# Small transfers of the inverse and of the sample step: from SyncE's DMA queue to GpSimd's

## The chip, the cores and the metric

The kernel runs on one core of one Trainium2 chip. The metric is the device time of one execution in microseconds (us). TensorE (PE) multiplies, VectorE (DVE) and ScalarE (ACT) do elementwise work, GpSimd (POOL) does some copies and issues DMAs, SyncE (SP) only issues DMAs.

## The reference, cut to what matters

Two layers of a hybrid decoder trunk over 256 prompt tokens and 8 sample tokens (264 columns in all). Each layer projects the normalised activations with one matrix, runs three branches on the result and projects back:

```python
for l in range(2):
    z = rms_norm(x) @ w_in[l]            # 2048 -> 3200 + 3072 + 1024 columns
    a = rwkv_time_mix(z[..., :3200], state_wkv[l], ...)   # 12 heads x 64, delta-rule matrix state
    b = attention_branch(z[..., 3200:6272], caches[l])    # 3 groups of 4 heads, windows 128, 512, 2048
    c = pool_branch(z[..., 6272:], state_pool[l])
    x = x + concat(a, b, c) @ w_out[l]   # 2048 -> 2048

def step(S, inp):                        # time mixing, one token
    sa = einsum('bhvk,bhk->bhv', S, -kk_t)
    S = S * w_t + sa[..., None] * (kk_t * a_t) + v_t[..., None] * k_t
    return S, einsum('bhvk,bhk->bhv', S, r_t)
```

The prompt's 256 time-mixing steps are done in four chunks of 64, which needs the inverse of a triangular 64x64 matrix for each of 12 heads and 4 chunks. The 8 sample tokens take one step each, from states in memory. Outputs are the activations, the new states and the new keys and values.

## The kernel before, in words

All weights are float32 in HBM. `stream` (L327 has its matmuls) loads them as 292 quarters of 512 KB (`raw`, three buffers, SP's queue, L155), ScalarE rounds each to `hi` (two buffers, L137), VectorE makes the rest `lo` = raw - hi (three buffers, L140), and 24 matmuls into `acc` read them: 7008 in all, 3504 a layer. Everything else on TensorE, here called side products, goes between these matmuls, into `a`. `w_out` is the last part of each layer's stream; its first quarter reads mb[1] and mb[2], the gated outputs of attention groups 1 and 2.

Time mixing in `a_solve`: chunk Gram matrices `gs` are stored to `g_dram`; the diagonal 32x32 blocks are loaded back as `xm`, with one row per block, and solved on VectorE column by column (`rm`, `tm`, 15 steps). The 16x16 inverses go through `rat_dram`, `ra_dram`, `rbt_dram` and `rb_dram` into the layout in which `invert` merges them on TensorE (product(x16, rat), then product(y16, right), then product(x32, rbt) and product(y32, rb)). x16 and x32 come back from `x_dram` and `x12_dram` in `load_x`. The result is stored in i22, i11 and i12 and loaded as `rt` by `inverses` for the chunk chain `turn`.

The sample step in `a_sample` spreads r, w, k and the others over partitions through `sk_dram` and `sv_dram`, loads them as `svec` and `sval`, updates the state in six pieces `s` (loaded and stored on GpSimd's queue, L158), and brings the output back through `so_dram` as `aos`. The sample attention stores its queries to `q_dram` and loads them as `qb`; keys and values come from the caches as `kc` and `vc`. In each group the products `a<-vc,ppad` feed VectorE's `ex` and `os`, ScalarE's `os`, two transposes on TensorE (L118), then `osb`, `sgb` and `mb`. GpSimd also copies the sample columns of queries, keys and values to `compb` (L855).

`dma` issues on SP (L155), `dma2` on GpSimd (L158). The order of instructions on each engine is not the order of the code: class `Plan` schedules the whole list with its own costs and dependences, and writes out one order for each engine, which the engine then keeps. A changed queue therefore moves other work too. `Plan` charges an issue on GpSimd's queue to GpSimd itself, and lets it land later than one on SP's.

Of the kernel before, what the change touches and what calls it, by code (L numbers as in the profile page):

```python
# [19 lines left out]
P = 128  # L20
# [83 lines left out]
class Trunk:  # L104
# [370 lines left out]
    def a_solve(self):  # L475

        ap = self.apool
        self.wc = ap.tile([P, 6, NCH], F32, tag="wc", name=self.nm("wc"))
        self.nc.gpsimd.tensor_copy(self.wc, self.wp[:, :, :, CH])
        xm, rm = (self.qpool.tile([P, 1056], F32, tag="s4", bufs=2, name=self.nm(s)) for s in ("xm", "rm"))  # L480
        tm = ap.tile([P, 768], F32, tag="k3", bufs=4, name=self.nm("tm"))
        mask = self.c("mask").unsqueeze(1).to_broadcast([P, NCH, P])
        for t0 in (0, 3):
            gs = [ap.tile([P, NH, P], F32, tag="gs", name=self.nm("gs"), bufs=2) for _ in UROWS]
            for i in range(3):
                pg = [self.ps("a") for _ in UROWS]
                with self.bundle(140):
                    for cidx in range(NCH):
                        for o, hr in zip(pg, UROWS):
                            self.mm(o[:, cidx * P:(cidx + 1) * P], self.bk[hr, t0 + i, cidx, :], self.ar[hr, t0 + i, cidx, :])  # L490
                for g, o in zip(gs, pg):
                    self.tt(g[:, 4 * i:4 * i + 4, :], o.rearrange("p (c n) -> p c n", n=P), mask, ALU.mult)
            for par, g in enumerate(gs):
                g0 = par * 6 + t0
                self.dma(self.g_dram[:, g0:g0 + 3].rearrange("p t c n -> p (t c n)"), g.rearrange("p h n -> p (h n)"))
                lo = slice(64 * par, 64 * par + 32)
                self.dma(self.x12_dram[4 * g0:4 * g0 + 12].rearrange("h s t -> s h t"), g[lo, :, 96:128])
        n = 96
        for blk in range(2):
            for par in range(2):  # L500
                r0, c0, q0 = 64 * par + 32 * blk, 64 + 32 * blk, 48 * blk + 24 * par
                self.dma(xm[q0:q0 + 24, :1024].rearrange("q (s x) -> q s x", x=32),
                         self.g_dram[r0:r0 + 32, 6 * par:6 * par + 6, :, c0:c0 + 32].rearrange("s t c x -> (t c) s x"))
        self.dma(self.x_dram, xm[:n, :1024])
        self.load_x()
        for par, hr in enumerate(UROWS):
            for t0 in (0, 3):
                g0 = par * 6 + t0
                self.dma(self.g_dram[hr, g0:g0 + 3].rearrange("p t c n -> p (t c) n")[:, :, 64:128],
                         self.ar[hr, t0:t0 + 3].rearrange("p t c n -> p (t c) n")[:, :, 64:128])  # L510
        view = lambda a: a[:n].rearrange("p (u x) -> p u x", u=2)[:, :, :512].rearrange("p u (s t) -> p u s t", t=32)[:, :, :, :16]
        X, R = view(xm), view(rm)
        self.nc.vector.memset(rm, 0.0)
        self.nc.vector.memset(rm[:, 0:1024:33], 1.0)
        for t in range(1, 16):
            tv = tm[:n, :2 * t * t].rearrange("p (u c s) -> p u c s", u=2, s=t)
            col = X[:, :, 0:t, t:t + 1].rearrange("p u s o -> p u o s").to_broadcast([n, 2, t, t])
            self.tt(tv, R[:, :, 0:t, 0:t], col, ALU.mult)
            self.red(R[:, :, 0:t, t:t + 1], tv)
        self.act(X.rearrange("p u s t -> p u t s"), R)  # L520
        for blk in range(2):
            rows = slice(48 * blk, 48 * blk + 48)
            self.dma(self.rat_dram[:, 1 - blk], X[rows, 0])
            self.dma(self.ra_dram[:, 1 - blk], R[rows, 1])
        self.nc.gpsimd.memset(xm[:48, :512].rearrange("p (s t) -> p s t", t=32)[:, :, 16:32], 0.0)
        self.dma(self.rbt_dram.rearrange("q s t -> q (s t)"), xm[:48, :1024])
        self.dma(self.rb_dram.rearrange("q s t -> q (s t)"), rm[48:96, :1024])

    def invert(self):

# [10 lines left out]
        self.dma(rbt, self.rbt_dram.rearrange("(g j) r t -> (j r) g t", j=4))  # L541
        self.dma(rb, self.rb_dram.rearrange("(g j) r t -> (j r) g t", j=4))
# [13 lines left out]
        p = product(self.x16, rat, 16)  # L556
# [9 lines left out]
        self.dma(self.i22_dram.rearrange("(g j) r t -> (j r) g t", j=4), rb)  # L566
# [5 lines left out]
        self.dma(self.i11_dram.rearrange("(i k) s j t -> (k s) i (j t)", k=4), inv[:, 0].rearrange("p (i n) -> p i n", i=3))  # L572
        p = product(y32, rb, 32)
        self.act(inv[:, 1].rearrange("p (g t) -> p g t", t=32), p)
        self.dma(self.i12_dram.rearrange("(g j) r t -> (j r) g t", j=4), inv[:, 1].rearrange("p (g t) -> p g t", t=32))

    def load_x(self):
        self.x16 = self.apool.tile([P, 12, 32], F32, tag="st", name=self.nm("x16"), bufs=2)
        self.x32 = self.apool.tile([P, 12, 32], F32, tag="st", name=self.nm("x32"), bufs=2)
        self.nc.gpsimd.memset(self.x16, 0.0)  # L580
        for j in range(4):
            for u in range(2):
                o = 32 * j + 16 * u
                src = self.x_dram[48 * (1 - u):48 * (1 - u) + 48].rearrange("(g j) (r c) -> j r g c", j=4, c=32)
                self.dma(self.x16[o:o + 16, :, 16 * u:16 * u + 16], src[j, 0:16, :, 16:32])
        self.dma(self.x32, self.x12_dram.rearrange("(g j) r c -> (j r) g c", j=4))

    def a_chain(self):

# [58 lines left out]
    def inverses(self):  # L648

        rt = self.apool.tile([P, 6, NCH, 64], F32, tag="rt", name=self.nm("rt"))  # L650
        flat = rt.rearrange("p t c n -> p (t c) n")
        for par in range(2):
            lo, hi = slice(64 * par, 64 * par + 32), slice(64 * par + 32, 64 * par + 64)
            self.nc.gpsimd.memset(flat[hi, :, 0:32], 0.0)
            for cidx in range(NCH):
                self.dma(rt[lo, :, cidx, 0:32], self.i11_dram[6 * par:6 * par + 6, :, cidx, :].rearrange("g s x -> s g x"))
            for d, r in ((self.i22_dram, hi), (self.i12_dram, lo)):
                self.dma(flat[r, :, 32:64], d[24 * par:24 * par + 24].rearrange("h s t -> s h t"))
        return rt

    def rows(self, cidx):
# [118 lines left out]
    def a_sample(self):  # L780
# [10 lines left out]
        self.dma(v[:, 0:48], self.sv_dram.rearrange("n e -> (n e)").rearrange("(p x) -> p x", p=P))  # L791
        src = I["state_wkv"][l].rearrange("b h v k -> (b h v k)").rearrange("(p x) -> p x", p=P)
        dst = self.outs["s_wkv"][l].rearrange("b h v k -> (b h v k)").rearrange("(p x) -> p x", p=P)
        nv = 8
        for pc in range(48 // nv):
            if pc % 2 == 0:
                vec = sp.tile([P, 5, 64], F32, tag="arows", name=self.nm("svec"))
                self.dma(vec, self.sk_dram.rearrange("q n r e -> q (n r) e").rearrange("q (p g) e -> g p q e", g=3)[pc // 2])
# [18 lines left out]
        self.dma(self.so_dram.rearrange("n e -> (n e)").rearrange("(p x) -> p x", p=P), out)  # L817
        os_ = sp.tile([112, 64], F32, tag="aos", name=self.nm("aos"))
        sa = v[:112, 0:64]
        self.nc.vector.memset(os_[32:64], 0.0)  # L820
        for par in range(2):
            self.dma(os_[64 * par:64 * par + 48], self.so_dram.rearrange("(n q) e -> q n e", q=2)[par])
# [1005 lines left out]
```

## Time and profile before

| | us |
|---|---|
| median of 3 runs | 1066.29 (1060.89, 1066.29, 1066.63) |
| profiled execution | 1064.51 |
| its span, first to last instruction | 1062.7 |
| TensorE busy | 1040.7 (98%) |
| VectorE busy | 856.7 (81%) |
| ScalarE busy | 546.7 (51%) |
| GpSimd busy | 141.7 (13%) |

The granted TensorE clock was 0.998 of full speed over the execution, the 2.4 GHz level. DMA-issuing instructions are not counted as busy, so GpSimd's and SP's share is more than the table shows. The profiled execution's time lies within the three runs. In layer 0 the column-by-column solve runs around 165 to 200 us, the inverse's first product on TensorE starts at 211.1 us and `w_out` at 442.84; in layer 1 the last two are at 739.0 and 965.98.

### The profile page before, as it was taken

How to read it: one execution, taken by the hardware profiler on the slowest of the kernel's cores; microseconds unless marked ns; L12 is line 12 of the kernel's file. 1: busy time of each engine (PE TensorE's matmuls, PEld its weight loads, DVE VectorE, ACT ScalarE, POOL GpSimd, SP SyncE). 2: the span in 40 equal slices, each digit the busy share in tenths (PEclk: the TensorE clock that was granted, in tenths of full speed). 3: DMA queues.
4: the chain of work that ended last, by engine and by line, in shares of the span. 5: the costliest groups of instructions: out<-in, count | busy, mean ns of one | idle time of the engine just before them, and what ended most of it. 6: DMA issues, size and time to landing. Idle time of an engine off the chain costs nothing.

```text
span 1062.7 us, 24484 instructions
## 1 busy us (share of the span) xinstructions
PE 1040.7 (98%) x9787; PEld 991.8 (93%) x9787; DVE 856.7 (81%) x1680; ACT 546.7 (51%) x930; POOL 141.7 (13%) x260
## 2 busy tenths in 40 slices
PE   9999999999999999999999999999999999999998
PEld 9899898989999898999999998989898998999998
DVE  7769978899799898766675799679998999897444
ACT  7546433454656664545455564334546566644332
POOL 0003210210012200011010142103100121010000
PEclk9999999999999999999999999999999999999999
DMA  8654487897646885677766545887976568766774
GB/s 281 189 172 146 140 249 225 238 265 219 192 153 198 281 256 181 209 222 232 228 214 192 165 128 185 236 233 220 251 227 184 165 208 278 240 219 197 227 226 148
DMA packets 151002, 223.63 MB, mean 210 GB/s; under 512 B 75888, under 2 KB 104960, under 8 KB 150872
## 3 DMA queue, kind: packets, MB, share of 16 engines
q1 hardware_dynamic: 142840, 196.40, 61.5%
q0 software_dynamic: 8048, 25.67, 7.3%
q8 instruction: 77, 1.26, 0.5%
q14 instruction: 37, 0.30, 0.1%
HBM read 198.55 MB, written 24.03 MB: 209 GB/s over the span
## 4 chain that ended last, share of the span: by engine, by line
PE 71%; DVE 15%; DMA 7%; ACT 3%; issue 3%; SPq 1%; DVEq 0%; ACTq 0%; POOLq 0%
PE acc L327 60%; PE a L115 8%; DVE lo L140 4%; DMA raw<-in_w_in 3%; PE a L118 2%; ACT hi L137 1%; DVE z L140 1%; DMA s<-in_state_wkv 1%; SPq L155 1%; DMA qb<-q_dram 1%; DVE bk L149 1%; DVE s L140 1%; DVE bk L140 1%; DMA selb<-in_cselb 1%; DVE tm L140 1%
## 5 line engine op out<-in xcount | busy, mean ns | idle before, releaser
L327 PE MATMUL acc<-xh,hi 128*128 128x264 f32 x1824 | 472.1, 289 | 7.3 <-ACT hi L137 4.3
L327 PE MATMUL acc<-xl,hi 128*128 128x264 f32 x1824 | 471.4, 289 | 0.0
L137 ACT ACTIVATE hi<-raw 128x1024 fp32r<-128x1024 f32 x292 | 309.0, 1058 | 313.1 <-PE acc L327 227.5
L140 DVE TENSOR_TENSOR lo<-raw,hi 128x1024 fp32r<-128x1024 f32 x292 | 356.5, 1221 | 140.3 <-ACT hi L137 139.2
L327 PEld LDWEIGHTS acc<-xh,hi 128*128 128x128 f32 x1824 | 343.5, 188 | 12.1 <-ACT hi L137 5.2
L327 PEld LDWEIGHTS acc<-xl,hi 128*128 128x128 f32 x1824 | 344.0, 189 | 6.8 <-issue 4.9
L327 PE MATMUL acc<-xh,lo 128*128 128x264 f32 x1824 | 295.0, 288 | 0.7 <-DVE lo L140 0.5
L327 PEld LDWEIGHTS acc<-xh,lo 128*128 128x128 f32 x1824 | 248.5, 189 | 6.4 <-issue 2.5
L140 DVE TENSOR_TENSOR z<-acc,rstd 128x264 f32<-128x264 f32 (+1 forms) x112 | 51.9, 466 | 8.6 <-PE acc L327 6.2
L327 PE MATMUL acc<-mb,hi 128*128 128x264 f32 x384 | 57.1, 284 | 0.0
L327 PEld LDWEIGHTS acc<-mb,hi 128*128 128x128 f32 x384 | 51.0, 188 | 0.0
L357 POOL COPY zcol<-z 128x9 f32<-128x9 f32 x50 | 21.0, 421 | 218.5 <-DVE z L140 196.7
L327 PE MATMUL acc<-mh,hi 128*128 128x264 f32 x192 | 49.0, 283 | 0.0
L327 PE MATMUL acc<-ml,hi 128*128 128x264 f32 x192 | 49.0, 283 | 0.0
L327 PEld LDWEIGHTS acc<-ml,hi 128*128 128x128 f32 x192 | 36.1, 188 | 0.0
L327 PEld LDWEIGHTS acc<-mh,hi 128*128 128x128 f32 x192 | 36.0, 188 | 0.0
L327 PE MATMUL acc<-mb,lo 128*128 128x264 f32 x192 | 33.8, 285 | 0.0
L327 PE MATMUL acc<-mc,hi 128*128 128x264 f32 x256 | 33.8, 284 | 0.0
L327 PE MATMUL acc<-mh,lo 128*128 128x264 f32 x192 | 33.6, 283 | 0.0
L327 PEld LDWEIGHTS acc<-mc,hi 128*128 128x128 f32 x256 | 32.2, 189 | 0.0
L327 PEld LDWEIGHTS acc<-mh,lo 128*128 128x128 f32 x192 | 27.6, 188 | 0.0
L327 PEld LDWEIGHTS acc<-mb,lo 128*128 128x128 f32 x192 | 27.5, 188 | 0.0
(356 smaller groups left out, 1297.5 us busy)
## 6 DMA issues: line engine op xcount, KB each, us to landing
raw<-in_w_in SPq DMA_DIRECT2D x228, 512.0 KB
raw<-in_w_out SPq DMA_DIRECT2D x64, 512.0 KB
g_dram<-gs SPq DMA_DIRECT2D x8, 768.0 KB
gs<-g_dram SPq DMA_DIRECT2D x8, 768.0 KB
kc<-in_cache_k_w POOLq DMA_DIRECT2D x12, 512.0 KB, 5.7
qb<-q_dram SPq DMA_DIRECT2D x12, 512.0 KB
vc<-in_cache_v_w POOLq DMA_DIRECT2D x12, 512.0 KB, 4.8
s<-in_state_wkv POOLq DMA_DIRECT2D x12, 256.0 KB, 4.9
```

The lines of the kernel that those rows point to most:

```text
L115: self.note(self.nc.tensor.matmul(out, lhsT, rhs, start=start, stop=stop))
L118: self.note(self.nc.tensor.transpose(out, in_, self.c("ident")[base:base + k, base:base + k]))
L137: self.nc.scalar.activation(out, in_, func, **kw)
L140: self.nc.vector.tensor_tensor(out, a, b, op=op)
L149: self.nc.vector.scalar_tensor_tensor(out, a, s, b, op0=op0, op1=op1)
L155: self.nc.sync.dma_start(out, in_)
L327: self.nc.tensor.matmul(accs[t][:, :T], a[:, kk, cs], b[k], start=first, stop=q == order[-1] and kk == nk - 1 and late == 1)
L357: self.nc.gpsimd.tensor_copy(self.zcol[:, :, a], z[:, NP - 1:T])
```

## The change

62 DMAs a layer go from `dma` to `dma2`, and nothing else in the code is edited: 4 x12 stores, 4 xm loads and the x_dram store of `a_solve`; the stores of rat, ra, rbt and rb (6) and their loads (4); 8 x16 loads and the x32 load; the stores of i22, i11 and i12 and the 12 rt loads; 10 sk and 2 sv stores; the sval load, 3 svec loads, the so store and 2 aos loads. The weight quarters, g_dram, q_dram, qb and the masks stay on SP.

```diff
-                self.dma(self.x12_dram[4 * g0:4 * g0 + 12].rearrange("h s t -> s h t"), g[lo, :, 96:128])
+                self.dma2(self.x12_dram[4 * g0:4 * g0 + 12].rearrange("h s t -> s h t"), g[lo, :, 96:128])
...
-                self.dma(xm[q0:q0 + 24, :1024].rearrange("q (s x) -> q s x", x=32),
+                self.dma2(xm[q0:q0 + 24, :1024].rearrange("q (s x) -> q s x", x=32),
...
-        self.dma(rat, self.rat_dram.rearrange("(g j) u r t -> (j u r) g t", j=4))
-        self.dma(ra, self.ra_dram.rearrange("(g j) u r t -> (j u r) g t", j=4))
+        self.dma2(rat, self.rat_dram.rearrange("(g j) u r t -> (j u r) g t", j=4))
+        self.dma2(ra, self.ra_dram.rearrange("(g j) u r t -> (j u r) g t", j=4))
...
-                self.dma(self.x16[o:o + 16, :, 16 * u:16 * u + 16], src[j, 0:16, :, 16:32])
+                self.dma2(self.x16[o:o + 16, :, 16 * u:16 * u + 16], src[j, 0:16, :, 16:32])
...
-                self.dma(rt[lo, :, cidx, 0:32], self.i11_dram[6 * par:6 * par + 6, :, cidx, :].rearrange("g s x -> s g x"))
+                self.dma2(rt[lo, :, cidx, 0:32], self.i11_dram[6 * par:6 * par + 6, :, cidx, :].rearrange("g s x -> s g x"))
...
-                self.dma(self.sk_dram[q].rearrange("(n q) r e -> q n r e", q=2)[par], r[:, q].unsqueeze(1).to_broadcast([48, 4, 64]))
-            self.dma(self.sv_dram.rearrange("(n q) e -> q n e", q=2)[par], r[:, 5])
+                self.dma2(self.sk_dram[q].rearrange("(n q) r e -> q n r e", q=2)[par], r[:, q].unsqueeze(1).to_broadcast([48, 4, 64]))
+            self.dma2(self.sv_dram.rearrange("(n q) e -> q n e", q=2)[par], r[:, 5])
...
```

SP's queue near the end of layer 1, before: the store of the sample queries, q_dram, stands between the weight quarters (raw with a number).

```order
L155 DMA raw_12408<-in_w_in 128x1024
L155 DMA raw_12438<-in_w_in 128x1024
L155 DMA q_dram<-brows_11655 48x3x128
L155 DMA raw_12468<-in_w_in 128x1024
L155 DMA qb_11696<-q_dram 128x4x256
L155 DMA raw_12539<-in_w_in 128x1024
L155 DMA msk_11436<-in_cmask 128x128
L155 DMA raw_12569<-in_w_in 128x1024
```

The same place of SP's queue in the changed kernel.

```order
L155 DMA raw_12438<-in_w_in 128x1024
L155 DMA raw_12468<-in_w_in 128x1024
L155 DMA raw_12539<-in_w_in 128x1024
L155 DMA raw_12569<-in_w_in 128x1024
L155 DMA q_dram<-brows_11655 48x3x128
L155 DMA msk_11436<-in_cmask 128x128
L155 DMA raw_12599<-in_w_in 128x1024
L155 DMA qb_11696<-q_dram 128x4x256
```

q_dram and the first qb load stand three weight quarters later. On TensorE, the changed kernel's w_out begins in layer 1 with mb_12935 (group 1) into acc_13258 and acc_13259; os_1855 and mb_12936 are those of group 2.

```order
L327 MATMUL acc_13258<-mb_12935,hi_13262 128x264
L327 MATMUL acc_13259<-mb_12935,hi_13262 128x264
L327 MATMUL acc_13258<-mb_12935,hi_13262 128x264 x2
L115 MATMUL a_11834<-vc_11835,ppad_11351 32x256 x4
L327 MATMUL acc_13258<-mb_12935,hi_13262 128x264
L327 MATMUL acc_13259<-mb_12935,hi_13262 128x264 x2
L115 MATMUL a_11834<-vc_11841,ppad_11351 32x256 x4
L327 MATMUL acc_13259<-mb_12935,hi_13262 128x264
L118 MATMUL a_11852<-cbase,os_1855_11849 128x128 x2
L327 MATMUL acc_13258<-mb_12936,hi_13262 128x264
L327 MATMUL acc_13259<-mb_12936,hi_13262 128x264
```

Before, the last os transposes (a_11852) and the last vc products stand ahead of w_out, the transposes by 15 weight matmuls; now both stand inside its first quarter. In layer 0 the transposes (a_4755, os_753) move from 37 weight matmuls ahead of w_out to 8. On GpSimd, the changed kernel has in layer 1, where before only the two compb copies and the stores out_s_wkv stood:

```order
L158 DMA x_1376_8710<-x_dram 16x12x16 x3
L855 COPY compb_7373<-z_9872 128x8
L158 DMA x_1376_8710<-x_dram 16x12x16 x2
L855 COPY compb_7373<-z_9874 128x8
L158 DMA x_1376_8710<-x_dram 16x12x16 x3
L158 DMA rat_9887<-rat_dram 128x12x16
L158 DMA ra_9888<-ra_dram 128x12x16
L158 DMA iv_9890<-rbt_dram 128x12x32
L158 DMA out_s_wkv<-s_1431_9209 128x512
```

The loads of x16, rat and ra now share a queue with GpSimd's copies. In layer 0 the order is seven x16 loads, a copy, the eighth x16, rat, a copy, ra.

## Rows read from the trace of the kernel before

**Rows 1.** the page: busy time, packets, and the chain that ended last by engine.

```profile
PE 1040.7 (98%) x9787; PEld 991.8 (93%) x9787; DVE 856.7 (81%) x1680; ACT 546.7 (51%) x930; POOL 141.7 (13%) x260
...
DMA packets 151002, 223.63 MB, mean 210 GB/s; under 512 B 75888, under 2 KB 104960, under 8 KB 150872
...
PE 71%; DVE 15%; DMA 7%; ACT 3%; issue 3%; SPq 1%; DVEq 0%; ACTq 0%; POOLq 0%
```

**Rows 2.** windows (us; busy per engine and instructions, clock, DMA share, GB/s), in the solve.

```profile
150.00:175.00 25.00, 23.79 (x197) 23.35 (x195) 18.22 (x42) 9.72 (x13) 2.63 (x7) 1.00 0.89 245
```

**Rows 3.** SP's timeline (start us, duration us, line, op, tiles, count), the solve of layer 0.

```profile
167.22 2.71 SPq L155 DMA_DIRECT2D sk_dram<-arows  x3
170.03 0.40 SPq L155 DMA_DIRECT2D raw<-in_w_in  x1
```

**Rows 4.** the chain in order of time (start, us, what), the same place.

```profile
170.03 3.94 DMA raw<-in_w_in
```

**Rows 5.** waits (us, times, longest) of 125 to 185 us, then 650 to 712.

```profile
PE acc L327 <- ACT hi L137: 2.3, 2, 1.4
...
PE acc L327 <- ACT hi L137: 2.0, 2, 1.2
```

**Rows 6.** GpSimd's groups by line and form (busy us, mean ns | idle before).

```profile
L158 POOL DMA_DIRECT2D kc<-in_cache_k_w x12 | 9.1, 757 | 27.4 <-DVE sct L152 14.4 <-DVE cd L140 9.9 <-DVE sc L1090 3.1
...
L158 POOL DMA_DIRECT2D out_s_wkv<-s x12 | 6.5, 546 | 53.5 <-DVE s L140 38.8 <-DVE nsq L140 11.0 <-DVE nwt L149 3.6
```

**Rows 7.** GpSimd's timeline, compb copies of layer 0, then of layer 1.

```profile
205.74 2.33 POOL L855 COPY compb<-z 128x8 f32<-128x8 f32 x1 [13.83 <-DVE z L140]
...
208.55 2.80 POOL L855 COPY compb<-z 128x8 f32<-128x8 f32 x1
...
730.92 8.21 POOL L855 COPY compb<-z 128x8 f32<-128x8 f32 x1 [0.73 <-DVE z L140]
```

**Rows 8.** tiles ra and rat (ns min/median/max, first and last start us), layers 0, 0, 1.

```profile
L155 SPq DMA_DIRECT2D ra<-ra_dram x1: 729/729/729, 207.1 to 207.1; - x1
...
L115 PE MATMUL a<-rat,x x96: 171/178/198, 211.1 to 214.6; 32*32 32x16 f32 x96
...
L115 PE MATMUL a<-rat,x x96: 171/178/199, 739.1 to 742.4; 32*32 32x16 f32 x96
```

**Rows 9.** ScalarE's timeline (in brackets: idle before, and its releaser), layer 0.

```profile
212.29 0.46 ACT L137 ACTIVATE ra<-ra,cbase 128x192 f32<-128x192 f32 x1 [1.00 <-DMA ra<-ra_dram]
```

**Rows 10.** SP's timeline near the end of layer 1's projection.

```profile
867.66 0.33 SPq L155 DMA_DIRECT2D q_dram<-brows  x1
...
877.96 0.33 SPq L155 DMA_DIRECT2D raw<-in_w_in  x1
```

**Rows 11.** tile ppad, layer 1.

```profile
L115 PE MATMUL a<-vc,ppad x48: 376/379/404, 938.3 to 958.4; 128*32 128x256 f32 x48
```

**Rows 12.** TensorE's timeline around w_out's start, layer 0, then layer 1.

```profile
438.12 0.38 PE L118 MATMUL a<-cbase,os 128*128 128x128 f32 x2
...
442.84 1.13 PE L327 MATMUL acc<-mb,hi 128*128 128x264 f32 x8
...
963.92 0.38 PE L118 MATMUL a<-cbase,os 128*128 128x128 f32 x2
...
965.98 1.15 PE L327 MATMUL acc<-mb,hi 128*128 128x264 f32 x8
966.96 0.28 PE L327 MATMUL acc<-mb,lo 128*128 128x264 f32 x1
```

**Rows 13.** VectorE's timeline at the same places, with ScalarE's os before the last.

```profile
441.38 0.77 DVE L140 TENSOR_TENSOR mb<-sgb,mb 128x264 fp32r<-128x264 f32 x2
...
958.84 0.69 DVE L140 TENSOR_TENSOR ex<-a,cbase 128x512 f32<-128x512 f32 x1
...
960.70 0.31 ACT L137 ACTIVATE os<-os 128x128 f32<-128x128 f32 x1 [0.46 <-DVE os L152]
...
965.38 0.78 DVE L140 TENSOR_TENSOR mb<-sgb,mb 128x264 fp32r<-128x264 f32 x2
```

More of the change, by code (lines that the diff above doesn't have):

```diff
@@ L501, in a_solve @@
                 r0, c0, q0 = 64 * par + 32 * blk, 64 + 32 * blk, 48 * blk + 24 * par
-                self.dma(xm[q0:q0 + 24, :1024].rearrange("q (s x) -> q s x", x=32),
+                self.dma2(xm[q0:q0 + 24, :1024].rearrange("q (s x) -> q s x", x=32),
                          self.g_dram[r0:r0 + 32, 6 * par:6 * par + 6, :, c0:c0 + 32].rearrange("s t c x -> (t c) s x"))
-        self.dma(self.x_dram, xm[:n, :1024])
+        self.dma2(self.x_dram, xm[:n, :1024])
         self.load_x()
@@ L522, in a_solve @@
             rows = slice(48 * blk, 48 * blk + 48)
-            self.dma(self.rat_dram[:, 1 - blk], X[rows, 0])
-            self.dma(self.ra_dram[:, 1 - blk], R[rows, 1])
+            self.dma2(self.rat_dram[:, 1 - blk], X[rows, 0])
+            self.dma2(self.ra_dram[:, 1 - blk], R[rows, 1])
         self.nc.gpsimd.memset(xm[:48, :512].rearrange("p (s t) -> p s t", t=32)[:, :, 16:32], 0.0)
-        self.dma(self.rbt_dram.rearrange("q s t -> q (s t)"), xm[:48, :1024])
-        self.dma(self.rb_dram.rearrange("q s t -> q (s t)"), rm[48:96, :1024])
+        self.dma2(self.rbt_dram.rearrange("q s t -> q (s t)"), xm[:48, :1024])
+        self.dma2(self.rb_dram.rearrange("q s t -> q (s t)"), rm[48:96, :1024])
     def invert(self):
@@ L538, in invert @@
         rb, rbt = pack[:, 0], pack[:, 1]
-        self.dma(rat, self.rat_dram.rearrange("(g j) u r t -> (j u r) g t", j=4))
-        self.dma(ra, self.ra_dram.rearrange("(g j) u r t -> (j u r) g t", j=4))
-        self.dma(rbt, self.rbt_dram.rearrange("(g j) r t -> (j r) g t", j=4))
-        self.dma(rb, self.rb_dram.rearrange("(g j) r t -> (j r) g t", j=4))
+        self.dma2(rat, self.rat_dram.rearrange("(g j) u r t -> (j u r) g t", j=4))
+        self.dma2(ra, self.ra_dram.rearrange("(g j) u r t -> (j u r) g t", j=4))
+        self.dma2(rbt, self.rbt_dram.rearrange("(g j) r t -> (j r) g t", j=4))
+        self.dma2(rb, self.rb_dram.rearrange("(g j) r t -> (j r) g t", j=4))
         m0, m1 = c("low")[:, 0:1], c("low")[:, 1:2]
@@ L565, in invert @@
         self.act(y32, p)
-        self.dma(self.i22_dram.rearrange("(g j) r t -> (j r) g t", j=4), rb)
+        self.dma2(self.i22_dram.rearrange("(g j) r t -> (j r) g t", j=4), rb)
         pt = self.ps("a")
@@ L571, in invert @@
         self.act(inv[:, 0], pt[:, :384])
-        self.dma(self.i11_dram.rearrange("(i k) s j t -> (k s) i (j t)", k=4), inv[:, 0].rearrange("p (i n) -> p i n", i=3))
+        self.dma2(self.i11_dram.rearrange("(i k) s j t -> (k s) i (j t)", k=4), inv[:, 0].rearrange("p (i n) -> p i n", i=3))
         p = product(y32, rb, 32)
         self.act(inv[:, 1].rearrange("p (g t) -> p g t", t=32), p)
-        self.dma(self.i12_dram.rearrange("(g j) r t -> (j r) g t", j=4), inv[:, 1].rearrange("p (g t) -> p g t", t=32))
+        self.dma2(self.i12_dram.rearrange("(g j) r t -> (j r) g t", j=4), inv[:, 1].rearrange("p (g t) -> p g t", t=32))
     def load_x(self):
@@ L584, in load_x @@
                 src = self.x_dram[48 * (1 - u):48 * (1 - u) + 48].rearrange("(g j) (r c) -> j r g c", j=4, c=32)
-                self.dma(self.x16[o:o + 16, :, 16 * u:16 * u + 16], src[j, 0:16, :, 16:32])
-        self.dma(self.x32, self.x12_dram.rearrange("(g j) r c -> (j r) g c", j=4))
+                self.dma2(self.x16[o:o + 16, :, 16 * u:16 * u + 16], src[j, 0:16, :, 16:32])
+        self.dma2(self.x32, self.x12_dram.rearrange("(g j) r c -> (j r) g c", j=4))
     def a_chain(self):
@@ L655, in inverses @@
             for cidx in range(NCH):
-                self.dma(rt[lo, :, cidx, 0:32], self.i11_dram[6 * par:6 * par + 6, :, cidx, :].rearrange("g s x -> s g x"))
+                self.dma2(rt[lo, :, cidx, 0:32], self.i11_dram[6 * par:6 * par + 6, :, cidx, :].rearrange("g s x -> s g x"))
             for d, r in ((self.i22_dram, hi), (self.i12_dram, lo)):
-                self.dma(flat[r, :, 32:64], d[24 * par:24 * par + 24].rearrange("h s t -> s h t"))
+                self.dma2(flat[r, :, 32:64], d[24 * par:24 * par + 24].rearrange("h s t -> s h t"))
         return rt
@@ L786, in a_sample @@
             for q in range(5):
-                self.dma(self.sk_dram[q].rearrange("(n q) r e -> q n r e", q=2)[par], r[:, q].unsqueeze(1).to_broadcast([48, 4, 64]))
-            self.dma(self.sv_dram.rearrange("(n q) e -> q n e", q=2)[par], r[:, 5])
+                self.dma2(self.sk_dram[q].rearrange("(n q) r e -> q n r e", q=2)[par], r[:, q].unsqueeze(1).to_broadcast([48, 4, 64]))
+            self.dma2(self.sv_dram.rearrange("(n q) e -> q n e", q=2)[par], r[:, 5])
         v = sp.tile([P, 96], F32, tag="sval", name=self.nm("sval"))
         out = v[:, 48:96]
-        self.dma(v[:, 0:48], self.sv_dram.rearrange("n e -> (n e)").rearrange("(p x) -> p x", p=P))
+        self.dma2(v[:, 0:48], self.sv_dram.rearrange("n e -> (n e)").rearrange("(p x) -> p x", p=P))
         src = I["state_wkv"][l].rearrange("b h v k -> (b h v k)").rearrange("(p x) -> p x", p=P)
@@ L797, in a_sample @@
                 vec = sp.tile([P, 5, 64], F32, tag="arows", name=self.nm("svec"))
-                self.dma(vec, self.sk_dram.rearrange("q n r e -> q (n r) e").rearrange("q (p g) e -> g p q e", g=3)[pc // 2])
+                self.dma2(vec, self.sk_dram.rearrange("q n r e -> q (n r) e").rearrange("q (p g) e -> g p q e", g=3)[pc // 2])
             vs = slice(pc * nv, pc * nv + nv)
@@ L816, in a_sample @@
             self.red(out[:, vs], tm)
-        self.dma(self.so_dram.rearrange("n e -> (n e)").rearrange("(p x) -> p x", p=P), out)
+        self.dma2(self.so_dram.rearrange("n e -> (n e)").rearrange("(p x) -> p x", p=P), out)
         os_ = sp.tile([112, 64], F32, tag="aos", name=self.nm("aos"))
@@ L821, in a_sample @@
         for par in range(2):
-            self.dma(os_[64 * par:64 * par + 48], self.so_dram.rearrange("(n q) e -> q n e", q=2)[par])
+            self.dma2(os_[64 * par:64 * par + 48], self.so_dram.rearrange("(n q) e -> q n e", q=2)[par])
         st = sp.tile([112, 4], F32, tag="ast", name=self.nm("ast"))
```

## The prediction

> **What bounds the kernel now.** I read the page's busy list and chain of waits first, then the stretches in which TensorE's sum falls short, then SP's and GpSimd's (POOL's) rows there. TensorE is busy 1040.7 of 1062.7 us and is 71% of the chain that ended last [rows 1]: it is a stream of weight matmuls, so a change can win at most the 22 us it stands still, and it loses whatever makes a matmul of the stream wait. The instruction order is fixed beforehand on every engine, so a late small product also stops the weight matmuls behind it. One stretch bears directly on the queue that is relieved: from 150 to 175 us TensorE lacks 1.2 of 25 us while the DMA engines are 0.89 busy [rows 2]. There SP's issues are backed up: the three sk_dram stores from 167.22 lasted 2.71 us, and the quarter behind them was issued only at 170.03 [rows 3]; its 3.94 us landing stands in the chain [rows 4]. TensorE waits for `hi`, the rounded copy of such quarters, 2.3 us in layer 0 and 2.0 us at the same place of layer 1 [rows 5]. That sum, 4.3 us, is what the relief of SP can give back.
>
> **SP loses 62 issues a layer.** Its free issues last some 0.3 to 0.4 us [rows 10]; none of this is on TensorE's path except where a quarter stands behind them, as above. With xm, x_dram, sk and sv gone, the quarters of the solve are issued when a buffer comes free. What stays ahead of them are the g_dram stores, and their landing on engines that are 0.89 busy. So the gain is 0 to 4.3 us; I take 3, since the rows show issue delay and landing in like parts (2.71 us of sk stores against 3.94 us of landing), and the quarter that follows has sk and sv stores ahead of it too. This is a gain: **-3 us** (0 to -4.3).
>
> **POOL gains 62 issues a layer.** One issue costs POOL 0.55 us where the transfer has 128 rows of destination and 0.76 us where it is a cache tile [rows 6]. At 0.55 to 0.76 us, 62 of them are 34 to 47 us per layer of an engine that is busy 141.7 of 1062.7 us: POOL does not become the bound as a whole, but within a chain each issue is 0.2 to 0.4 us later than on SP, and it stands in line with POOL's copies. The place where that counts is the loads of the inverse. There POOL now issues x16, a compb copy, x16, a second compb copy, then x16, rat, ra (the third order block above). These copies of 8 columns can be held for long: 2.33 and 2.80 us in layer 0, 8.21 us in layer 1 [rows 7]. POOL's own DMA issues, out_s_wkv's from the same stretches among them, keep their 0.55 us [rows 6], so I charge only the copies. Landing: the ra load of before, issued on SP at 207.1 for 0.73 us, was awaited by ScalarE until 212.29, so 4.5 us [rows 8, 9]. No row has such a load on POOL, so I take the same and count the issue delay alone.
>
> In layer 0 the copies of before ended at 208.07 and 211.35 [rows 7]. With the rat load between them, at 208.1 plus one x16 (0.55), it is issued by 209.2 and lands 4.5 us on, at 213.7; the first product that reads rat started at 211.1 [rows 8]: 2.6 us late. ra, behind the second copy, is issued about 212.5 and lands at 217, where ScalarE used it at 212.29: 4.7 us late [rows 9], and the `right` operand of the next product hangs on it. In layer 1, if the second copy is held again for 8.21 us it ends at 739.1; three x16 and rat follow (four times 0.55), so rat is there at 739.1 + 2.2 + 4.5 = 745.8, where the product began at 739.0: 6.8 us [rows 8]. If the copy is not held, the five loads after it begin at 731 and nothing is late. So this is 2.6 to 4.7 us in layer 0 and 0 to 6.8 us in layer 1. Half of the second is 3.4 us, and the product is itself placed a little later in the new order; I take 3 in each layer: **+6 us** (0 to 11.5). It has no bound from above in one respect: after it come the stores of the inverse, i11, i22 and i12, and the twelve rt loads, all on POOL. Twelve rt issues at 0.55 to 0.76 take 6.6 to 9.1 us against about 4 on SP (0.33 each). That is 2.6 to 5.1 us more per layer in the chunk chain, hidden only if the order leaves this much room; the order has put the chunk products later, so I add nothing to the middle, and 5 us to the upper end.
>
> **The end of layer 1: w_out's first quarter.** The new order puts q_dram's store three weight quarters later (first order block). Before, it was issued at 867.66; the third of those quarters was issued at 877.96, so the store now follows 878.3: 10.6 us later [rows 10]. Everything of the sample attention hangs on it, to the last pair of os transposes. TensorE's program answers: the last vc products, which ended at 958.4 + 0.4, now stand four to seven matmuls *inside* w_out, whose first matmul was at 965.98 [rows 11, 12]; at 0.12 us a matmul (the ninth of w_out starts at 966.96, eight after the first) that is 966.8, so 8.0 to 8.4 us later. The slot moved less than its input: 10.6 - 8.4 = 2.2 us of lateness if the attention had no room, 0 if it had that much. Behind the last product stands **one** weight matmul, then the os transposes, and directly behind these the products that read mb_12936 (second order block). Before, the time between was full of weight matmuls; now nothing is there. What lies between is in the rows: from the product's end at 958.8, VectorE's ex and os follow, then ScalarE's os until 960.70 + 0.31 = 961.0, 2.2 us [rows 13]; from the transposes' end at 963.92 + 0.38 = 964.30, osb, sgb and the two mb, which end at 965.38 + 0.78 = 966.16, 1.9 us [rows 12, 13]. So TensorE must stop 2.2 + 1.9 - 0.12 = 4.0 us at this point even if every input is on time, and up to 6.2 us with the lateness. I take **+5 us** (4.0 to 6.2). Before, it did not wait there at all: mb was ready at 966.16 and its first reader, the fifth matmul, came at 965.98 + 4 x 0.12 = 966.5.
>
> **The end of layer 0.** The same transposes stood at 438.12, 4.7 us ahead of w_out's first matmul at 442.84 [rows 12]. They move to eight matmuls ahead of it, and eight mb_5838 products follow before the first that needs them: 16 x 0.12 = 1.9 us of cover. The work between took 1.9 us in layer 1; in layer 0, with `lo` of the next quarter in front, it ended at 441.38 + 0.77 = 442.15, 3.65 us after the transposes' end [rows 13]. So 0 to 1.7 us; I take **+1 us**.
>
> **Sum.** 1064.5 (the profiled execution; its span is 1062.7) - 3 + 6 + 5 + 1 = 1073.5. That execution stands 0.2% under the median of the runs shown, 1066.29, and within them; I forecast 1074, about 0.7% over the median. Every other edit (sval, svec, so and aos, x12 and xm) I take as nothing: they are hidden by the stream as long as their products are placed with room, and their cost if not is the same 0.2 to 0.4 us per issue.
>
> **Rivals.**
> *Faster.* The relief of SP is all that counts: at the solve the weights come on time, 4.3 us, and the orders at w_out cost nothing because the attention before ran far ahead of its slot. For it: TensorE never waits there now. Against it: the 4.0 us between product and reader does not depend on how early the inputs are. It would decide if the solve also gave back landing time of quarters; 1064.5 - 4.3 = 1060, or 1062 with a part of the w_out stop. Chance 0.10.
> *No gain and little loss.* The backed-up issues of the solve come from the 16 DMA engines and not from SP: 75,888 of 151,002 packets are under 512 B [rows 1], and these remain. Then the -3 is 0; if the inverse has 3 us of room per layer too, only w_out's 4 us remain, and with the 1 us of layer 0 at most 1069. The Trainium skill, "DMA: Bandwidth & Descriptors", section "Issuing engines are not separate DMA queues", says so as a rule: whichever engine issues, the transfers run on the same 16 engines, and only issue time is saved. By it the share of 0.89 would stay; the rows on SP at 167 us show that issue time is also at stake, so I give it part of the weight. 1065 to 1069, chance 0.15.
> *Much slower.* The blocked copy in layer 1 holds the rat and ra loads for 8 us as it did out_s_wkv's, and the rt loads come 5 us late in each layer: 1064.5 + 4.7 + 6.8 + 10 + 6 = 1092. For it: the 8.21 us row. Against it: it depends on which VectorE operation the copy meets. Chance 0.13.
>
> **How the numbers follow.** The forecast has 0.62, of which 0.07 ends inside 0.5% (5.3 us, about what a measurement of this kernel can tell from no change). So faster 0.10, same 0.15 + 0.07 = 0.22, slower 0.13 + 0.55 = 0.68. The range runs from 1063, which leaves the better half of the fast case out, to 1090, just short of the last sum.
>
> **What would show it.** In the new trace TensorE should stop 4 us or more at the os transposes inside w_out of layer 1, waiting on `os` and `mb`, and about 1 us in layer 0; its waits for `hi` near 173 and 698 us should be gone or halved; compb copies of over 2 us should stand ahead of the rat and ra issues, with ScalarE or TensorE waiting on these loads. If there is no stop at w_out, the forecast fails by its surest term; if rat and ra are on time in both layers, the time is about 1068.

## The result and the profile after

The changed kernel takes 1081.63 us (median of 3 runs, 1080.51 to 1082.58) against 1066.29: a ratio of 1.0154, 95% interval 1.0128 to 1.0180, so 15 us slower. The forecast was 1074. The profiled execution of the changed kernel took 1080.51 us, its span is 1078.6, 15.9 us more than before. The page shows where to look; these lines answer [rows 1].

```profile
PE 1044.6 (97%) x9787; PEld 996.0 (92%) x9787; DVE 857.6 (80%) x1680; ACT 546.4 (51%) x930; POOL 212.2 (20%) x384
...
DMA packets 95322, 223.64 MB, mean 207 GB/s; under 512 B 18256, under 2 KB 47264, under 8 KB 95192
```

TensorE is busy 3.9 us more and idle 12.0 us more (34.0 against 22.0), with the same number of matmuls. So most of the loss is standing still, and a part is the same work done more slowly. GpSimd's count rises from 260 to 384, by the 124 transfers that moved: on this engine the page counts the issues as busy, before as well. By their groups in the trace these 124 took 84.5 us, 0.68 us each, 42 us a layer, inside the forecast's 34 to 47. The second line says that of the packets under 512 B, which the forecast expected to stay, three quarters are gone. TensorE's timeline shows the stops that the kernel before did not have (in brackets the idle time before the row, and its releaser):

```profile
144.51 1.89 PE L115 MATMUL a<-ar,bk 64*128 64x128 f32 x14 [2.40 <-DVE zv L149]
...
431.38 1.08 PE L115 MATMUL a<-vc,ppad 128*32 128x256 f32 x8 [2.13 <-DMA vc<-in_cache_v_w]
...
452.40 0.76 PE L327 MATMUL acc<-mb,hi 128*128 128x264 f32 x4 [1.11 <-DVE mb L140]
...
973.48 0.98 PE L327 MATMUL acc<-mb,hi 128*128 128x264 f32 x4 [1.10 <-ACT mb L137]
...
979.42 0.44 PE L118 MATMUL a<-cbase,os 128*128 128x128 f32 x2 [2.95 <-ACT os L137]
980.96 1.71 PE L327 MATMUL acc<-mb,hi 128*128 128x264 f32 x6 [1.10 <-ACT mb L137]
```

Together these are 2.40 + 2.13 + 1.11 + 5.15 = 10.8 us. The reader should see that three stand where the forecast put them: 1.11 us at w_out of layer 0, and 2.95 and 1.10 us at the last os transposes and group 2's mb in layer 1. Three do not: the one at the Gram products of the solve in layer 0, the one at a vc product, and the 1.10 us ahead of w_out's first matmul in layer 1, which waits for group 1's mb. Behind the long ones the granted clock falls. These are windows of the changed kernel (us; busy time and instructions of PE, PEld, DVE, ACT, POOL; granted clock; DMA share; GB/s):

```profile
144.70:148.10 3.40, 3.40 (x22) 3.18 (x21) 2.37 (x4) 0.00 (x0) 1.19 (x2) 0.50 0.75 229
431.40:434.80 3.40, 3.40 (x19) 2.59 (x20) 2.18 (x3) 0.14 (x1) 0.75 (x1) 0.50 0.68 194
981.00:984.30 3.30, 3.30 (x15) 3.30 (x16) 0.72 (x2) 0.44 (x2) 0.00 (x0) 0.50 0.00 0
```

Each is a stretch of about 3.4 us at 0.50, the 1.2 GHz level; before, there is one such stretch early in the execution, and the changed kernel has that one too. TensorE had stood still for 2.1 to 3.0 us shortly before each fell. At half clock 3.4 us do the work of 1.7, so three stretches cost 5.1 us, most of which shows as the 3.9 us of busy time. The new stops and these 5.1 us add up to the 15.9 us of the span; all other gains and losses cancel.

What holds the Gram products: VectorE may not overwrite `gs` before both its stores have landed. Tile x_dram in the changed kernel (durations in ns, first and last start, who waited, landing), and then VectorE's row in the kernel before and in the changed one:

```profile
L158 POOL DMA_DIRECT2D x_dram<-gs x4: 618/634/767, 133.3 to 152.3; - x4
...
  DVE gs L140: 4.0, 1
...
DMA to landing us min/median/max: 5.8/7.1/7.8
```

```profile
137.62 0.69 DVE L140 TENSOR_TENSOR gs<-a,cbase 128x512 f32<-128x512 f32 x1 [0.88 <-DMA x_dram<-gs]
...
140.81 0.69 DVE L140 TENSOR_TENSOR gs<-a,cbase 128x512 f32<-128x512 f32 x1 [3.98 <-DMA x_dram<-gs]
```

The views leave numbers out of names, so x12_dram stands there as x_dram; what is stored from gs is x12. The x12 stores of layer 0, the first of them issued at 133.3 us in both kernels, land 5.8 to 7.8 us after their issue in the changed one. VectorE waits 3.98 us for one where it waited 0.88 us for the store on SP before, and TensorE then waits for VectorE. In layer 1 VectorE waits 1.4 us at the same place and TensorE 0.4. The waits of TensorE in the solve, layer 0 and then layer 1, answer [rows 5]:

```profile
PE a L118 <- DVE z L140: 0.7, 2, 0.5
PE acc L327 <- DVE lo L140: 0.6, 1, 0.6
PE acc L327 <- ACT hi L137: 0.2, 1, 0.2
...
PE acc L327 <- DVE lo L140: 1.7, 2, 0.9
PE acc L327 <- DVE z L140: 1.0, 1, 1.0
PE a L118 <- DVE z L140: 0.3, 1, 0.3
```

The waits for `hi` fell from 4.3 to 0.2 us, but waits for `lo` and `z` of 4.3 us stand in their place, where before only 0.5 us for `lo` stood in layer 1. Whether the relief of SP's queue did this is taken up with order_before_sample_pool below. The loads of the inverse (GpSimd's timeline, layers 0 and 1) answer [rows 7, 8]:

```profile
208.03 0.59 POOL L855 COPY compb<-z 128x8 f32<-128x8 f32 x1 [4.72 <-DVE z L140]
...
209.09 1.03 POOL L158 DMA_DIRECT2D rat<-rat_dram  x1
210.12 0.69 POOL L855 COPY compb<-z 128x8 f32<-128x8 f32 x1
210.75 1.03 POOL L158 DMA_DIRECT2D ra<-ra_dram  x1
...
740.43 0.23 POOL L855 COPY compb<-z 128x8 f32<-128x8 f32 x1
```

The copies took 0.23 to 0.69 us here, not 2.3 to 8.2. VectorE ran two-operand work all the same; these are its rows on both sides of the copy of 0.23 us:

```profile
739.92 0.68 DVE L140 TENSOR_TENSOR s<-sval,svec 128x512 f32<-128x512 f32 x1
740.52 1.22 DVE L140 TENSOR_TENSOR lo<-raw,hi 128x1024 fp32r<-128x1024 f32 x1
```

What parts these copies from the long ones no run shows. One of these loads costs GpSimd 1.03 us to issue, more than the 0.55 to 0.76 of the forecast. ScalarE did wait for ra:

```profile
217.31 0.46 ACT L137 ACTIVATE ra<-ra,cbase 128x192 f32<-128x192 f32 x1 [2.00 <-DMA ra<-ra_dram]
```

but the product that hangs on it came later still, and TensorE did not stop in the inverse.

### The profile page after: what moved, and what is told of

Read it like the earlier page. It is cut to its first block, busy times and chain, and to the rows that moved or that the text cites. A ratio compares the mean times of both kernels' runs of the same rounds, so it can differ in the third digit from the quotient of the medians.

```text
span 1078.6 us, 24521 instructions
## 1 busy us (share of the span) xinstructions
PE 1044.6 (97%) x9787; PEld 996.0 (92%) x9787; DVE 857.6 (80%) x1680; ACT 546.4 (51%) x930; POOL 212.2 (20%) x384
## 2 busy tenths in 40 slices
DMA packets 95322, 223.64 MB, mean 207 GB/s; under 512 B 18256, under 2 KB 47264, under 8 KB 95192
## 4 chain that ended last, share of the span: by engine, by line
PE 45%; DVE 8%; DMA 3%; ACT 2%; issue 2%; POOL 0%; SPq 0%; DVEq 0%; ACTq 0%; POOLq 0%
PE acc L327 40%; PE a L115 3%; DVE lo L140 3%; DMA g_dram<-gs 1%; PE a L118 1%; ACT hi L137 1%; DMA raw<-in_w_in 1%; DMA xm<-g_dram 1%; DVE gs L140 1%; DMA vc<-in_cache_v_w 1%; DVE z L140 0%; DVE bk L149 0%; DVE bk L140 0%; DVE r L149 0%; DVE ls L441 0%
## 5 line engine op out<-in xcount | busy, mean ns | idle before, releaser
L327 PE MATMUL acc<-mb,hi 128*128 128x264 f32 x384 | 59.6, 289 | 3.4 <-ACT mb L137 2.2
L158 POOL DMA_DIRECT2D resid<-xs x16 | 8.7, 542 | 100.8 <-DVE xs L140 100.8
```

Source lines behind the costliest of these rows:

```text
L158: self.nc.gpsimd.dma_start(out, in_)
L327: self.nc.tensor.matmul(accs[t][:, :T], a[:, kk, cs], b[k], start=first, stop=q == order[-1] and kk == nk - 1 and late == 1)
```

## The experiments

`Plan` makes a new order whenever a queue changes, so undoing a part changes two things at once. For most of the kernels below the two are held apart: a transfer is planned as if on one queue and issued on the other. TensorE's, VectorE's and ScalarE's orders then are row for row those of the kernel named; the transfers are put into the real queue's order by their planned start.

```diff
+    def cross(self, queue, out, in_): self.crossed.add(queue.dma_start(out, in_).ins.name)
...
-        self.eng = [engine(i) for i in self.ins]
+        self.real = [engine(i) for i in self.ins]; self.eng = [{'SP': 'POOL', 'POOL': 'SP'}[e] if i.name in crossed else e for i, e in zip(self.ins, self.real)]
...
-        for ks in self.order.values():
+        for ks in [[k for k in sorted(range(self.n), key=lambda k: (self.start[k], k)) if self.real[k] == e] for e in self.order]:
```

Ratios are to runs of the kernel before on the same chip, with their 95% interval; 4 to 12 executions of each kernel, 3 of the changed one.

| kernel | median us | ratio | interval |
|---|---|---|---|
| changed kernel | 1081.63 | 1.0154 | 1.0128 to 1.0180 |
| order_before_queue_pool | 1087.17 | 1.0196 | 1.0162 to 1.0230 |
| order_after_queue_sp | 1070.52 | 1.0038 | 1.0021 to 1.0055 |
| order_after_x12_sp | 1072.80 | 1.0063 | 1.0041 to 1.0084 |
| after_wout_0123 | 1073.52 | 1.0063 | 1.0031 to 1.0094 |
| order_after_queue_sp_wout | 1067.02 | 1.0015 | 0.9992 to 1.0037 |
| before_wout_0123 | 1066.52 | 1.0008 | 0.9987 to 1.0029 |
| order_after_x12_sp_wout | 1074.05 | 1.0076 | 1.0050 to 1.0102 |
| sample_only | 1072.60 | 1.0058 | 1.0041 to 1.0075 |
| inverse_only | 1079.21 | 1.0113 | 1.0084 to 1.0142 |
| order_before_x12_pool | 1070.54 | 1.0046 | 1.0028 to 1.0064 |
| order_before_sample_pool | 1072.65 | 1.0065 | 1.0041 to 1.0089 |
| order_before_but_x12_pool | 1078.34 | 1.0127 | 1.0102 to 1.0153 |

**Queue without order, order without queue.** My theory after the trace was that the new order, with its stops at w_out, costs more than the queue.

```diff
-                self.dma(self.x12_dram[...], g[lo, :, 96:128])
+                self.cross(self.nc.gpsimd, self.x12_dram[...], g[lo, :, 96:128])    # order_before_queue_pool, and so for all 124
+                self.cross(self.nc.sync, self.x12_dram[...], g[lo, :, 96:128])      # order_after_queue_sp, planned as dma2
```

> The 124 transfers go out on GpSimd, but every engine's order is that planned for the kernel before (TensorE, VectorE and ScalarE have its order row for row). Theory, most of the 15 us comes with the new order: no stop inside w_out; the stop at the second pair of gs products in layer 0 is there, since the x12 store lands late whatever the order (2.4 us, and a stretch at half clock of some 1.3 us after it); the weight waits of 4.3 us in the solve are gone; the inverse, placed for quicker loads, stops 0 to 3 us a layer: 1066 to 1071, so -0.1% to +0.5%. Rival, the queue itself costs: the late landings stop TensorE wherever they are awaited, 1076 to 1084.

> The reverse: every engine's order is that planned for the changed kernel, but the 124 transfers go out on SP. Theory, the order costs: inside w_out of layer 1 TensorE still stops 1.1 + 2.95 + 1.1 us, in layer 0 1.1 us, the wait for vc at 431 us (2.1 us) stays, each long stop is followed by a half-clock stretch worth about 1.3 us; the gs stop (2.4 us and its half clock) goes: 1072 to 1077. Rival, the queue costs: 1062 to 1068.

The theory fell. With the order of before, the queue alone costs 2.0%; with the new order on SP only 0.4% is lost. So the queue costs about 21 us in the one order and 12 us (1.0154 - 1.0038) in the other. The new order costs 4 us with the transfers on SP; with them on GpSimd it costs nothing that can be seen (1.0154 against 1.0196, and the intervals overlap). In the first of the two the trace shows the main part of the forecast's much slower rival, the held copy; the rt loads, for which that rival charged 10 us, stopped TensorE for 1.4. GpSimd, layer 1:

```profile
742.43 7.84 POOL L855 COPY compb<-z 128x8 f32<-128x8 f32 x1
...
751.28 1.03 POOL L159 DMA_DIRECT2D rat<-rat_dram  x1
752.30 1.02 POOL L159 DMA_DIRECT2D ra<-ra_dram  x1
```

TensorE, and its window behind the stop:

```profile
757.88 0.84 PE L115 MATMUL a<-rat,x 32*32 32x16 f32 x24 [7.69 <-DMA ra<-ra_dram]
```

```profile
757.80:768.00 10.20, 10.12 (x128) 9.29 (x129) 4.00 (x14) 2.91 (x6) 5.04 (x6) 0.50 0.63 144
```

A copy held for 7.84 us delays rat and ra, TensorE stops 7.69 us at the first product of the inverse, and some 10 us at half clock follow. That the loads behind the copy make the stop is seen in sample_only below, where a copy is held for 7.61 us at the same place, rat and ra come on SP, and TensorE does not stop. While the copy was held VectorE ran only two-operand work, until the reduction with which the copy ended at 750.27:

```profile
743.04 0.68 DVE L140 TENSOR_TENSOR s<-asa,svec 128x512 f32<-128x512 f32 x1
...
750.13 0.67 DVE L152 TENSOR_REDUCE sval<-s 128x8 f32<-128x512 f32 x1
```

The Trainium skill, "SBUF — State Buffer", section "Who interferes with whom", says that a VectorE instruction with two SBUF inputs contends with a GpSimd instruction that reads SBUF, and that a reduction does not; this trace agrees, with a hold of 7.84 us that ended 0.14 us after the reduction began. It does not tell when such work holds a copy: the copy of 0.23 us in the changed kernel had two-operand instructions on both sides. In order_after_queue_sp the stops at w_out of layer 1 stay (TensorE's waits, and the clock behind them):

```profile
PE a L118 <- ACT os L137: 2.9, 1, 2.9
PE acc L327 <- ACT mb L137: 2.2, 2, 1.1
```

```profile
966.70:973.50 6.80, 5.93 (x27) 5.93 (x28) 2.40 (x6) 1.80 (x3) 0.00 (x0) 0.50 0.00 0
```

These are 5.1 us of stops and 6.8 us at half clock. They belong to the order, as the forecast said. The vc wait of 2.13 us at 431 us, which the expectation kept, is not there, so in this order it came with the queue. Until it reached w_out of layer 1 that execution was 6 us ahead of the profiled execution of before (its first matmul there started at 960.1, against 965.98), which is why its net loss is small. That lead is not all of the order's making: this execution, at 1067.87 us, is the fastest of the 12, and it lacks the early stretch at half clock that the kernel before and the changed one have, worth 1.7 us.

**The x12 stores.**

> The changed kernel with its own order; the 8 x12 stores alone go out on SP. Theory, the late landing of the x12 store holds the two gs buffers and so VectorE and TensorE: the 2.40 us stop at 144.5 us falls below 0.5 us and the half clock behind it goes, 3 to 4 us faster than the changed kernel, 1078. Rival, another thing holds the gs product (the g_dram store of the same buffer, 768 KB): no change, 1081 to 1083.

The edit leaves the changed kernel's order and issues the 8 x12 stores on SP. The ratio falls from 1.0154 to 1.0063, about 9 us and more than the 3 to 4 expected. The g_dram stores of the same buffers are as they were, so the rival is out. VectorE's wait and the clock around 144 us:

```profile
137.61 0.69 DVE L140 TENSOR_TENSOR gs<-a,cbase 128x512 f32<-128x512 f32 x1 [0.95 <-DMA x_dram<-gs]
```

```profile
141.00:148.00 7.00, 7.00 (x71) 6.46 (x70) 5.27 (x9) 1.30 (x2) 1.34 (x2) 1.00 0.65 166
```

The stop and the half clock of layer 0 are gone: at this point the execution is 4.7 us ahead of the changed kernel's. By 185 us it is 6.1 ahead. At the vc wait it wins another 2.3, since the wait is 1.35 instead of 2.13 us and no half clock follows it; at w_out of layer 1 it loses 1.1, since the half clock there lasts 6.8 us instead of 3.4; at the end 7.8 us are left. So 8 of 124 transfers carry most of what the queue costs in this order, about half of it directly at the Gram products; why the rest follows is not shown. Over all the kernels of the table the stop goes with these stores: with x12 on GpSimd four of five profiled executions have it, at 2.40 or 2.41 us, and with x12 on SP none does. The reverse, x12 alone on GpSimd in the order of before:

> The kernel before with its own order; the 8 x12 stores alone go out on GpSimd. Theory: their late landing is enough for the stop at the gs products of layer 0 (2.4 us) and a half-clock stretch behind it (3.4 us long, so 1.7 us lost): 1069 to 1071, 4 to 5 us over the kernel before. Rival, alone on GpSimd's queue they land as soon as on SP: 1064 to 1067.

The time is as the theory said, 0.46% or 5 us. Its trace does not show the cause: the profiled execution took 1066.59 us, the second of 12 in speed (nine took 1069.5 to 1073.4), and in it VectorE waited less than in the changed kernel, and TensorE not at all for it. The stores did land late, 4.8 to 8.3 us after issue in layer 0, though of the moved transfers they alone are on that queue:

```profile
138.93 0.69 DVE L140 TENSOR_TENSOR gs<-a,cbase 128x512 f32<-128x512 f32 x1 [1.42 <-DMA x_dram<-gs]
```

> The kernel before with its own order; all 124 transfers but the 8 x12 stores go out on GpSimd. Theory: of the 21 us of order_before_queue_pool the stop at the first product of the inverse in layer 1 remains (7.7 us behind a compb copy of 7.84 us, and 13.65 us at half clock behind it, 6.8 us lost): 1078 to 1083. Rival, the copy is held by chance and is not held this time: 1066 to 1070.

1078 us, as the theory said, and the stop is the same one:

```profile
751.82 0.84 PE L115 MATMUL a<-rat,x 32*32 32x16 f32 x24 [7.31 <-DMA ra<-ra_dram]
```

The 6.8 us that the expectation charged for half clock are too many: in order_before_queue_pool the stretch began at 754.7 us, while TensorE stood still until 757.88.

**Distance at w_out.**

```diff
-            accs = self.stream(I["w_out"][l], 256 * j, 2, self.mhs, self.mls, (2, 1, 3, 0))
+            accs = self.stream(I["w_out"][l], 256 * j, 2, self.mhs, self.mls, (0, 1, 2, 3))
```

> The changed kernel with w_out's quarters read in the order 0, 1, 2, 3 (was 2, 1, 3, 0), planned anew: the attention outputs of groups 1 and 2 are first read 48 matmuls (5.8 us) later in the stream. Theory, the 5.2 us of stops in layer 1 and 1.1 us in layer 0 are a missing distance between producer and reader: they go, and with them the half clock of layer 1, 5 to 7 us faster than the changed kernel, 1074 to 1077. Rival, the planner gives the room away again by placing the attention later still: 1080 to 1083.

1073.52, 8 us better than the changed kernel, by the ratio (1.0063) the same as for the x12 stores; the stops at w_out shrink, though in layer 1 a vc product and mb are still waited for (TensorE's timeline), and no half clock follows:

```profile
973.21 0.64 PE L115 MATMUL a<-vc,ppad 128*32 128x256 f32 x8 [1.81 <-DMA vc<-in_cache_v_w]
...
981.32 1.46 PE L327 MATMUL acc<-mb,hi 128*128 128x264 f32 x8 [1.22 <-ACT mb L137]
```

> The kernel before with w_out's quarters in the order 0, 1, 2, 3, a control. Theory: TensorE never waited at w_out there, so nothing is to be won: 1064 to 1068. Rival: the new order of quarters is itself worth several us: below 1062 or above 1070.

1066.52, no difference to the kernel before, so the order of quarters has no worth of its own; it is worth something where the attention ends late.

> As order_after_queue_sp (1070.5 us), with w_out's quarters read in the order 0, 1, 2, 3. Theory: that run was 6 us ahead of the kernel before when it came to w_out of layer 1 and lost 9 there, 1.10 + 2.94 + 1.09 us of stops and 6.8 us at half clock; with the distance restored it keeps the 6 us: 1059 to 1062, faster than both kernels. Rival, planning anew puts the attention later and the stops come back, or the 6 us were of that one order: 1065 to 1071.

1067.02: the rival. The stops of layer 1 shrink to a vc wait of 1.0 and an mb wait of 1.2 us, but planned anew most of the lead is not there (0.3 us between the layers, where order_after_queue_sp had 2.8). It is level with the kernel before and no version beats it.

> The changed kernel with w_out's quarters in the order 0, 1, 2, 3, planned as such; the 8 x12 stores alone go out on SP. Theory: both named losses are gone, the gs stop and the stops in w_out: 1064 to 1068, level with the kernel before. Rival, planning anew takes it back as it did in order_after_queue_sp_wout: 1069 to 1073.

1074.05: the expectation's rival again, and a little above its range. The two mends, 8 to 9 us each when made alone, do not add up. Its trace has no gs stop, but four stretches at half clock behind the early one; the longest stop ahead of each is 0.9 to 2.3 us, and the mean clock of the execution is 0.992, against 0.998 before.

**One half at a time.** Here the edits of the diff are made in `a_sample` only, or everywhere else only.

> Only the sample step's 18 transfers a layer go to GpSimd (sk, sv, sval, svec, so, aos); x12, xm, x16, rat, ra, rt stay on SP; planned anew. Theory: the sk and sv stores leave the queue of the weight quarters in the solve, nothing waits for their landing early, no gs stop: 1062 to 1069. Rival, any small transfer that lands later costs, wherever it is: 1072 or more.

> Only the 44 transfers a layer of the inverse go to GpSimd, x12 and xm among them; the sample step stays on SP; planned anew. Theory: the x12 landing stops VectorE and TensorE at the gs products of layer 0 (2.4 us and half clock behind it): 1072 to 1080. Rival, the sample step's half brought the loss: 1064 to 1068.

inverse_only fits the theory: the gs stop is there, and others, the two longest of which are these (the execution shown, at 1074.61 us, is the fastest of 6):

```profile
143.13 1.13 PE L115 MATMUL a<-ar,bk 64*128 64x128 f32 x14 [2.41 <-DVE zv L149]
...
260.41 0.69 PE L118 MATMUL a<-cbase,bk 128*128 128x128 f32 x2 [2.42 <-DVE st L140]
...
451.93 1.41 PE L327 MATMUL acc<-mb,hi 128*128 128x264 f32 x6 [1.71 <-ACT mb L137]
```

sample_only does not, its time is the rival's: 6 us slower, with no gs stop. Its largest stop is one for weights, in the solve that it was to relieve:

```profile
176.58 0.39 PE L327 MATMUL acc<-xh,hi 128*128 128x264 f32 x1 [2.82 <-ACT hi L137]
```

To part order from queue there too:

> The kernel before with its own order; the sample step's 36 transfers alone go out on GpSimd. Theory: none of them is awaited early, the 6 us of sample_only came from its new order: 1063 to 1067, with the weight waits of the solve (4.3 us) smaller. Rival, the sample step's transfers themselves delay something: 1070 or more.

1072.65, the rival. Just ahead of the sample attention of layer 1 the profiled execution was 0.8 us behind the kernel before; nearly all of the rest is one stop at a vc product, with 6.8 us at half clock behind it:

```profile
953.58 1.08 PE L115 MATMUL a<-vc,ppad 128*32 128x256 f32 x8 [4.39 <-DMA vc<-in_cache_v_w]
```

```profile
940.41 0.75 POOL L158 DMA_DIRECT2D vc<-in_cache_v_w  x1 [22.74 <-PE a L115]
946.76 0.75 POOL L158 DMA_DIRECT2D vc<-in_cache_v_w  x1 [5.60 <-DVE lo L140]
```

The second vc load of the pair was issued 6.4 us after the first, where before it was 4.7, and landed 6.8 us after issue, where before the loads of this stretch took 3.9 to 4.4: issued at 944.39 us, this one was awaited at 948.44 and had no margin. Why moving transfers of the sample step, 150 us earlier, should make it late is open, and vc waits of 1 to 2 us appear in several kernels, on SP too. The run also answers the forecast's -3: the sk and sv stores are off SP here, in the order of before, and TensorE waits for `hi` longer, 5.8 us in place of 4.3 (its waits at the places of [rows 5], layers 0 and 1):

```profile
PE acc L327 <- ACT hi L137: 3.5, 2, 1.9
...
PE acc L327 <- ACT hi L137: 2.3, 1, 2.3
```

In order_after_queue_sp, with all of them on SP, it waits 2.0 us in layer 0 and not at all in layer 1. So the sk and sv stores ahead of the quarters were not what made the quarters late, and part of the fall to 0.2 us in the changed kernel is the order's.

## Why the prediction was wrong

The direction was right and the time lies in the stated range, but the size was half of what was measured: +7.7 us forecast, +15.3 measured. That it lies in the range is in part luck. Of the sum's +9 over the profiled execution, the two terms for w_out came, 6.3 us; the -3 and the +6 did not. On top came 9.6 us that the sum had at nothing: a stop of 2.4 us from the x12 stores, one of 2.1 us at a vc product, and 5.1 us of half clock.

- *The end of layer 1, +5.* The mechanism is right: at the place that was worked out, the os transposes and group 2's mb, TensorE stops 2.95 + 1.10 = 4.05 us, the 4.0 of the working, and the lateness added to it (up to 2.2 us) did not come. The total of 5.15 is near 5 by luck: the first 1.10 us is at group 1's mb, which the working did not look at. That the order makes these stops is shown by order_after_queue_sp, where they stay with all transfers on SP.
- *The end of layer 0, +1.* Right, 1.11 us.
- *The solve, -3.* Wrong. The `hi` waits went (4.3 to 0.2 us), but `lo` and `z` were next in line with 4.3 us, and nothing was won. Nor was the cause the one named: with the sk and sv stores alone off SP the `hi` waits grew to 5.8 us (order_before_sample_pool).
- *The inverse, +6.* Did not come, TensorE did not stop there, since the copies were not held; why they were not is open, for VectorE ran two-operand work beside them too. The mechanism and its size (6.8 us forecast, 7.69 measured) are shown by order_before_queue_pool, where a copy is held. An issue of rat or ra took 1.03 us, not 0.55.
- *"Every other edit (sval, svec, so and aos, x12 and xm) I take as nothing."* This is the step that failed. The x12 store frees a gs buffer, VectorE waits for that buffer within microseconds, and on GpSimd's queue it lands 5.8 to 7.8 us after issue. The working looked for loads that somebody waits for and not for stores that give a buffer back, and it priced a moved transfer at the 0.2 to 0.4 us of its issue, not at its landing. In the changed kernel's trace this costs the stop of 2.40 us and 1.7 us of half clock; putting these 8 stores back is worth 9 of the 15 us.
- *A term that was not in the sum:* behind the three longest places of waiting the clock was at 0.50 for 3.4 us. These stretches lost 5.1 us. The forecast counted each stop at its own length.
- *The vc wait,* 2.13 us, was not foreseen either. It is gone when the transfers go out on SP in the same order, and 1.35 us when x12 alone does; how the queue makes it is not settled.
- *No gain and little loss,* the rival with the small packets, is refuted in its time, and in one premise: the small packets did not remain (75,888 to 18,256). The load hardly changed, as it said: from 150 to 175 us the DMA engines' share is 0.86 against 0.89. What it left out is that the moved stores land later.

That stops, waits and half clock do not simply add is shown by the two mends; each new plan brings stops of a few us in places of its own, of which I can explain only those named.

## What to carry to other kernels

When a store moves to a queue on which it lands later, ask who waits for the buffer that it reads from, not only who reads what it writes. Reckon with a stretch at half clock behind a stop of TensorE; here it cost 1.7 us behind stops of 2.1 to 3.0 us. Where a planner orders all engines, hold its order while the queue changes, and the reverse: each part has another price beside the other, and their sum tells neither.

## What the runs showed of the hardware

The queues' packets, MB and share of the 16 DMA engines' span, before and then in the changed kernel:

```profile
q1 hardware_dynamic: 142840, 196.40, 61.5%
q0 software_dynamic: 8048, 25.67, 7.3%
...
q1 hardware_dynamic: 82008, 186.96, 55.6%
q0 software_dynamic: 13200, 35.12, 11.0%
```

The same transfers that took 60,832 packets of the hardware queue took only 5,152 more of the software queue. Their time fell much less: by these shares, an estimate, from 54 to 41 us of the 16 engines. And they land later: an x12 store 5.8 to 7.8 us after issue. The issue took 1.03 us for rat and ra, against 0.62 to 0.77 us for an x12 store.

The stretches at half clock lasted 3.4 us behind stops of about 1 to 3 us, 6.8 us behind the stops at w_out of order_after_queue_sp and behind the 4.39 us stop, and 10 and 14 us around the two stops of over 7 us, the first 2 to 3 us of them before TensorE went on. Not every stop brought one: the 2.82 us of sample_only and the 1.81 us of after_wout_0123 did not, and inverse_only has one, from 420.9 us, with no stop in the 20 us ahead of it. What parts these is open.
